# Dilated attention on tokens in order of their residues, and unsplit first modulation rows

## The chip, the cores and the metric

The kernel runs on one core of a Trainium2 chip as one program. The metric is the device time in microseconds, the median of several runs. Of the kernel before, three runs took 3383.66, 3390.68 and 3393.23 us.

## The reference, cut to what matters

The program is two transformer blocks one after the other over 512 tokens of width 1024, in float32. The first block has two layers, each with modulation by a condition vector, attention over 512 tokens and 256 context tokens, and a mixture of experts. The part of it that matters here is the first line: `silu` of two condition vectors (for tokens and for context) times 2048 columns of `mod_w[0]` gives a shift and a scale, and the layer begins with them.

```python
mods  = (silu_c  @ mod_w[i] + mod_b[i]).reshape(b, 1, 6, d)          # six rows of 1024
cmods = (silu_cc @ mod_w[i][:, :n_cm*d] + mod_b[i][:n_cm*d])         # the same for the context
a_lat = modulate(h_lat, mods[:, :, 0], mods[:, :, 1])                # x * (1 + scale) + shift
```

The second block normalises `x` to `h`, and feeds three branches with `h @ w_in`: gated linear attention, a short convolution, and dilated attention. Sigmoid gates `h @ w_gate + b_gate` weigh the branches; then come an output product and a feed-forward part.

```python
z = rmsnorm(x, pre_mix_g[l]) @ w_in[l]
y_gla, y_sc = gla_branch(...), sc_b * causal_dwconv(sc_c * sc_x, sc_conv_w[l])
y_dil = dilated_branch(d_q, d_k, d_v, positions)                     # 4 heads, 3 groups
gates = sigmoid(h @ w_gate[l] + b_gate[l]).reshape(B, S, 3, D_MODEL)
merged = sum(gates * einsum('bsgc,gcd->bsgd', [y_gla, y_sc, y_dil], w_branch[l]), axis=2)
```

Each head of the dilated branch has three groups, which are softmaxes of their own, joined by their denominators: one over near tokens (distances up to 128), and two over tokens whose distance is a multiple of four. `strided_window_attn` gathers the tokens of one residue modulo four with `t.reshape(B, L, dil, H, D).transpose(0, 2, 3, 1, 4)`.

## The kernel before, in words

Matrices lie with the inner dimension on the 128 partitions, so a width of 1024 is KC = 8 chunks. Most products are three matmuls (`mm3`, lines 239 to 243): each operand is split into a rounded part and a rest (`split`, L247 on ACT, L248 on DVE), and hi times hi, lo times hi and hi times lo are added in PSUM. `Stream` (from line 34) brings weights to raw slots by SP's DMA queue, in the order of a plan; a load into a slot waits until the slot was read. `get` gives split weights, `plain` unsplit ones.

The code makes instructions in program order, with generators that mix two bodies of work; a scheduler then sets the order on each engine from its own estimates. Each engine runs its list strictly in order.

At the start, `first_mods` (L326) reads 32 pieces of 256 KB of `mod_w` through 6 slots; each is split, and multiplied by the two condition columns in two matmuls (L339, L340). The row is copied out, transposed in 16 small pieces, and gives `mcol`, the shift and scale by partition (L349, L350). Then tokens `x` are transposed, modulated (L459, L460), and multiplied by the first attention weights `k_ab`, whose loads (L66) stand behind all pieces of `mod_w` in SP's queue.

In the second block `hTh` and `hTl` hold the split, transposed `h` (128 partitions x 8 chunks x 512 tokens). `gla` and `short_conv` run interleaved (`both`, L131), followed by `dilated`. There `project` makes, for the heads in pairs, V of each of three groups: for 128 tokens at a time, stationary operand `hTh[:, k, tokens]` or `hTl`, moving operand 256 weight columns, so 48 matmuls for each PSUM tile of 2 x 256 and 96 for each group and pair of heads. For groups 1 and 2 the tokens are `slice(b + i, 512, 4)`, every fourth one. Q and K are 128 x 512 tiles by head and group, turned by `rope_tables`. `scores(r)` handles the queries of residue r: one product with 512 keys (group 0, L2218) and two with 128 (L2220); with float32 operands each is two matmul instructions. `values(r)` writes the result into `yTh[:, h, r::4]`. After that gates and branches alternate: two gate tiles with a sigmoid (L1847) from PSUM, then two branch products `pb`; both kinds take PSUM tiles of tag `mm`, of which there are two.

Of the kernel before, what the change touches and what calls it, by code (L numbers as in the profile page):

```python
# [13 lines left out]
F32 = mybir.dt.float32  # L14
# [9 lines left out]
P = 128  # L24
D = 1024
# [158 lines left out]
class Kern:  # L184
# [121 lines left out]
    def silu_c(self, ps, pool, cr, sr):  # L306
# [7 lines left out]
        self.c2 = pool.tile([P, KC, 2, 2], FR, name="c2")  # L314
        c2 = pt[:, :16].rearrange("p (w k) -> p k w", w=2)
        self.split(self.c2[:, :, 0], self.c2[:, :, 1], c2)
# [10 lines left out]
    def first_mods(self, st, ps, row, cols):  # L327

        nc, A = self.nc, self.A
        pc = ps.tile([P, KC, 8], F32, tag="aux", name="pc")  # L330
        for j in (1, 0):
            nc.gpsimd.dma_start(row[4:5], A["mod_b"][0:1, j * D:(j + 1) * D])

            pm = [ps.tile([P, 512], F32, tag="mm", name="pm")[:4] for _ in range(2)]
            for k in range(KC):
                c = self.c2[:, k].rearrange("p x w -> p (x w)")
                for n in range(2):
                    h, l = st.get()
                    nc.tensor.matmul(pm[n], c, h[:, 0], start=k == 0, stop=False)  # L339
                    nc.tensor.matmul(pm[n][:2], c[:, :2], l[:, 0], start=False, stop=k == KC - 1)  # L340
                yield
            for n in range(2):
                nc.scalar.activation(row[:4, n * 512:(n + 1) * 512], pm[n], AF.Copy)
            for k in range(KC):
                self.transpose(pc[:, k, :5], row[:, k * P:(k + 1) * P])
            t = cols.rearrange("p (k c) -> p k c", k=KC)
            nc.scalar.activation(t, pc[:, :, :5], AF.Copy)
            m = self.mcol[:, 0, j]
            nc.vector.scalar_tensor_tensor(m, t[:, :, 0:2], float(j), t[:, :, 2:4], op0=OP.add, op1=OP.add)  # L349
            nc.vector.tensor_add(m, m, t[:, :, 4:5].to_broadcast([P, KC, 2]))  # L350
# [181 lines left out]
    def mixer_ab(self, atp, then):  # L532
        nc, tc, A, cp = self.nc, self.tc, self.A, self.cp
        NT, NB = NLAT + NCTX, 6
        with ExitStack() as es:
# [13 lines left out]
            wp = ws.enter_context(tc.tile_pool(name="m0w", bufs=1))  # L549
            plan = self.mod_plan(0, (1, 0))  # L550
# [13 lines left out]
            self.silu_c(ps, mp, xc[:16, 4096:4224], xc[:16, 4224:4352])  # L564
            st = Stream(self, wp, plan, 6, 6, 768)
            for i, _ in enumerate(self.first_mods(st, ps, xc[:5, 2048:3072], xc[:, 3072:3112])):
                if i == 12:
                    load_x(0)
# [1849 lines left out]
```

## Time and profile before

| | |
|---|---|
| runs | 3383.66, 3390.68, 3393.23 us |
| profiled execution | 3393.14 us, span 3391.4 us |
| busy | PE 90%, PEld 66%, DVE 45%, ACT 30%, POOL 17% |
| DMA | 647 MB, 191 GB/s on average |
| granted clock of PE, mean | 0.960 |

PE means matmuls, PEld the loads of the stationary operand, which overlap matmuls. A matmul's row shows its whole duration, but the next one starts before it ends; so the pace is read from the distance of two starts. In the rows a line number is the line of a helper where the helper makes the instruction: 241 to 243 are the three matmuls of every split product, told apart by their tiles. In the text below "k" is a chunk of 128 of the width. A row of the timeline ends with the idle time ahead of it and who ended that, where there was any.

### The profile page before, as it was taken

How to read it: one execution, taken by the hardware profiler on the slowest of the kernel's cores; microseconds unless marked ns; L12 is line 12 of the kernel's file. 1: busy time of each engine (PE TensorE's matmuls, PEld its weight loads, DVE VectorE, ACT ScalarE, POOL GpSimd, SP SyncE). 2: the span in 40 equal slices, each digit the busy share in tenths (PEclk: the TensorE clock that was granted, in tenths of full speed). 3: DMA queues.
4: the chain of work that ended last, by engine and by line, in shares of the span. 5: the costliest groups of instructions: out<-in, count | busy, mean ns of one | idle time of the engine just before them, and what ended most of it. 6: DMA issues, size and time to landing. Idle time of an engine off the chain costs nothing. (4 is left out here: it accounts for less than half of the span.)

```text
span 3391.4 us, 50303 instructions
## 1 busy us (share of the span) xinstructions
PE 3067.6 (90%) x18965; PEld 2233.6 (66%) x18965; DVE 1519.4 (45%) x3415; ACT 1010.7 (30%) x2201; POOL 592.6 (17%) x557
## 2 busy tenths in 40 slices
PE   7999999799999928998799989399999999979998
PEld 3677757455555527887555545188889888858887
DVE  5578866443222257755521212344533333365533
ACT  5455561111111015654111111133232332233321
POOL 1101012243422232011222111100031300010000
PEclk9999999799999968999799999799999999979999
DMA  7433142899999641113697999722121112412232
GB/s 255 157 99 105 62 165 106 350 393 418 392 418 419 283 145 34 51 42 116 265 399 288 418 417 403 263 85 73 46 75 50 69 63 93 150 75 100 100 118 75
DMA packets 146160, 647.13 MB, mean 191 GB/s; under 512 B 27890, under 2 KB 35586, under 8 KB 85586
## 3 DMA queue, kind: packets, MB, share of 16 engines
q1 hardware_dynamic: 120802, 597.84, 45.6%
q0 software_dynamic: 22224, 36.24, 3.4%
q10 hardware_dynamic: 2848, 9.19, 0.7%
q8 instruction: 186, 3.05, 0.4%
q14 instruction: 100, 0.82, 0.1%
HBM read 669.98 MB, written 35.03 MB: 208 GB/s over the span
## 5 line engine op out<-in xcount | busy, mean ns | idle before, releaser
L1597 PE MATMUL u<-raw,xs 128*64 128x256 f32 x5312 | 597.5, 382 | 18.9 <-DMA raw<-in_k_w 18.5
L1597 PEld LDWEIGHTS u<-raw,xs 128*64 128x64 f32 x5312 | 378.5, 137 | 219.1 <-DMA raw<-in_k_w 22.6
L248 DVE TENSOR_TENSOR wl<-raw,wh 128x2048 fp32r<-128x2048 f32 (+3 forms) x178 | 278.6, 1573 | 434.8 <-ACT wh L247 433.2
L247 ACT ACTIVATE wh<-raw 128x2048 fp32r<-128x2048 f32 (+3 forms) x180 | 239.1, 1335 | 416.1 <-PE pm L242 187.9
L241 PE MATMUL pm<-hTh,wh 128*128 128x512 f32 x872 | 344.8, 395 | 1.6 <-DVE hTl L248 1.4
L243 PE MATMUL pm<-hTh,wl 128*128 128x512 f32 x872 | 341.5, 392 | 1.1 <-DVE wl L248 1.1
L242 PE MATMUL pm<-hTl,wh 128*128 128x512 f32 x872 | 341.7, 392 | 0.0
L1617 PE MATMUL y<-raw,gs 128*64 128x512 f32 x1328 | 300.4, 598 | 4.2 <-ACT gs L1612 1.5
L1602 DVE TENSOR_TENSOR sg<-sg,u 128x256 f32<-128x256 f32 x132 | 55.5, 421 | 513.0 <-PEq L1650 293.4
L243 PE MATMUL pm<-wh,aTl 128*128 128x384 f32 (+2 forms) x576 | 201.1, 349 | 7.7 <-POOL aTl L461 7.5
L241 PE MATMUL pm<-wh,aTh 128*128 128x384 f32 (+2 forms) x576 | 203.5, 354 | 2.1 <-ACT aTh L460 2.0
L1617 PEld LDWEIGHTS y<-raw,gs 128*64 128x64 f32 x1328 | 88.9, 136 | 169.5 <-issue 155.4
L242 PE MATMUL pm<-wl,aTh 128*128 128x384 f32 (+2 forms) x576 | 198.8, 345 | 0.2 <-DVE wl L248 0.2
L1623 DVE SCALAR_TENSOR_TENSOR ys<-y,rt_sw,gate 128x512 f32<-128x512 f32 x128 | 93.5, 748 | 226.1 <-PE y L1617 226.1
L1601 ACT ACTIVATE sg<-u 128x256 f32<-128x256 f32 x132 | 50.6, 384 | 482.5 <-PE u L1597 315.8
L241 PEld LDWEIGHTS pm<-hTh,wh 128*128 128x128 f32 x872 | 163.9, 188 | 37.5 <-DVE hTl L248 1.8
L243 PEld LDWEIGHTS pm<-hTh,wl 128*128 128x128 f32 x872 | 163.6, 188 | 36.4 <-DVE wl L248 1.5
L242 PEld LDWEIGHTS pm<-hTl,wh 128*128 128x128 f32 x872 | 163.8, 188 | 34.5
L1612 ACT ACTIVATE gs<-t 128x512 f32<-128x512 f32 x66 | 39.4, 598 | 332.2 <-PE t L271 302.2
L1295 POOL DMA_INDIRECT xg<-f_d,rt_row x64 | 67.0, 1046 | 395.1 <-PE t L271 359.3
L271 PE MATMUL t<-ident,p 128*128 128x128 f32 x704 | 122.0, 284 | 6.0 <-ACT pT L885 1.0
L243 PEld LDWEIGHTS pm<-wh,aTl 128*128 128x128 f32 x576 | 114.3, 198 | 14.6 <-POOL aTl L461 9.2
(561 smaller groups left out, 5632.0 us busy)
## 6 DMA issues: line engine op xcount, KB each, us to landing
raw<-in_k_w SPq DMA_DIRECT2D x408, 1024.0 KB
raw<-in_k_sb SPq DMA_DIRECT2D x79, 1024.0 KB
raw<-in_mod_w SPq DMA_DIRECT2D x192, 256.0 KB
raw<-in_k_ab SPq DMA_DIRECT2D x24, 384.0 KB
raw<-in_k_cd SPq DMA_DIRECT2D x24, 384.0 KB
raw<-in_k_w_out SPq DMA_DIRECT2D x8, 1024.0 KB
raw<-in_k_sb SPq DMA_DIRECT2D x12, 512.0 KB
f_d<-f POOLq DMA_DIRECT2D x10, 512.0 KB, 2.9
```

What stands on the lines that cost most here:

```text
L241: nc.tensor.matmul(out, lh, rh, start=start, stop=False)
L242: nc.tensor.matmul(out, lh, rl, start=False, stop=False)
L243: nc.tensor.matmul(out, ll, rh, start=False, stop=stop)
L247: self.nc.scalar.activation(h, x, AF.Copy)
L248: (sub or self.nc.vector).tensor_sub(l, x, h)
L271: self.nc.tensor.transpose(out, in_, self.ident[:k, :k])
L1295: self.nc.gpsimd.indirect_dma_start(out=x, out_offset=None, in_=self.f_d[:nb * P], in_offset=bass.IndirectOffsetOnAxis(ap=gi, axis=0), bou ...
L1597: nc.tensor.matmul(pu[c][i][64 * n:64 * n + 64], xs[:, k, tok], w[:, k % 4, n * 256:(n + 1) * 256], start=k == 0, stop=k == KC - 1)
L1601: nc.scalar.activation(sg[c], pu[c][0], AF.Silu)
L1602: nc.vector.tensor_mul(sg[c], sg[c], pu[c][1])
L1617: nc.tensor.matmul(py[c][64 * n:64 * n + 64], gs[:, c, k % 2, k // 2], W[k // 2][:, k % 2, n * 512:(n + 1) * 512], start=k == 0, stop=k == 3)
L1623: nc.vector.scalar_tensor_tensor(y, py[c], sw[:, 0], gate[:, 0], op0=OP.mult, op1=OP.mult)
```

## The change

There are two parts. In the first, the 2048 columns for the first modulation come as 8 pieces of 1 MB, laid out ahead of time (`k_mod`), through 5 slots in a pool of its own. They are used unsplit in float32, with four column groups of 32 rows by 256 columns (`mod_row`, L325 to 329). The bias comes by POOL's DMA queue, and the row is transposed in two pieces. The pool of the six slots for `k_ab` opens after that pool is closed and covers its memory. In the second part, `hTh` and `hTl` are brought into the order of residues in place: each chunk is copied to a spare tile `turn` with a strided read, and back; `hTh` on ACT and `hTl` on POOL, in four further steps of `short_conv`. V of groups 1 and 2 and the queries of `scores` then take contiguous tokens; positions and masks follow that order (the masks lie where `gla` had its V), and the sigmoid of the gates, which still works on `h`, writes its result back to the natural order, with a stride of four. The writes to `yTh` stay.

```diff
@@ -324,30 +322,36 @@
-    def first_mods(self, st, ps, row, cols):
+    def mod_row(self, pm, k, w, last):
+
+        for q in range(4):
+            self.nc.tensor.matmul(pm[q * 32:q * 32 + 32], self.c2f[:, 2 * k:2 * k + 32], w[:, q * 256:(q + 1) * 256],
+                                  start=k == 0, stop=k == last)
+
+    def first_mods(self, ps, pool, then):
...
+        bias = pool.tile([P, 2, KC], F32, name="bias")
+        nc.gpsimd.dma_start(bias, A["k_mod_b"])
+        st = Stream(self, pool, [(Flat(A["k_mod"][i], 2),) for i in range(8)], 5, 0)
         for j in (1, 0):
-            nc.gpsimd.dma_start(row[4:5], A["mod_b"][0:1, j * D:(j + 1) * D])
-
-            pm = [ps.tile([P, 512], F32, tag="mm", name="pm")[:4] for _ in range(2)]
+            pm = ps.tile([P, 512], F32, tag="mm", name="pm")[:, :256]
             for k in range(KC):
-                c = self.c2[:, k].rearrange("p x w -> p (x w)")
-                for n in range(2):
-                    h, l = st.get()
-                    nc.tensor.matmul(pm[n], c, h[:, 0], start=k == 0, stop=False)
-                    nc.tensor.matmul(pm[n][:2], c[:, :2], l[:, 0], start=False, stop=k == KC - 1)
-                yield
-            for n in range(2):
-                nc.scalar.activation(row[:4, n * 512:(n + 1) * 512], pm[n], AF.Copy)
-            for k in range(KC):
-                self.transpose(pc[:, k, :5], row[:, k * P:(k + 1) * P])
-            t = cols.rearrange("p (k c) -> p k c", k=KC)
-            nc.scalar.activation(t, pc[:, :, :5], AF.Copy)
-            m = self.mcol[:, 0, j]
-            nc.vector.scalar_tensor_tensor(m, t[:, :, 0:2], float(j), t[:, :, 2:4], op0=OP.add, op1=OP.add)
-            nc.vector.tensor_add(m, m, t[:, :, 4:5].to_broadcast([P, KC, 2]))
+                if k % 2 == 0:
+                    w = st.plain()
+                self.mod_row(pm, k, w[:, k % 2], KC - 1)
+            row = pool.tile([P, 256], F32, tag="row", name="row", bufs=2)
+            nc.scalar.activation(row, pm, AF.Copy)
+            pc = ps.tile([P, 512], F32, tag="aux", name="pc")
+            for c in range(2):
+                self.transpose(pc[:, c * P:(c + 1) * P], row[:, c * P:(c + 1) * P])
+
+            for c in range(2):
+                m, b = (v.rearrange("p (q c) w -> p c q w", c=2)[:, c] for v in (self.mcol[:, 0, j], bias[:, j, :, None].to_broadcast([P, KC, 2])))
+                nc.vector.scalar_tensor_tensor(m, pc[:, c * P:(c + 1) * P].rearrange("p (q x) -> p q x", q=4)[:, :, 0:2], float(j), b,
+                                               op0=OP.add, op1=OP.add)
+            if j:
+                then()
@@ -546,8 +550,7 @@
             ws = ent(ExitStack())
-            wp = ws.enter_context(tc.tile_pool(name="m0w", bufs=1))
-            plan = self.mod_plan(0, (1, 0))
+            plan = []
@@ -562,10 +565,10 @@
             self.silu_c(ps, mp, xc[:16, 4096:4224], xc[:16, 4224:4352])
+            with tc.tile_pool(name="m0f", bufs=1) as fp:
+                self.first_mods(ps, fp, lambda: load_x(0))
+            wp = ws.enter_context(tc.tile_pool(name="m0w", bufs=1))
             st = Stream(self, wp, plan, 6, 6, 768)
-            for i, _ in enumerate(self.first_mods(st, ps, xc[:5, 2048:3072], xc[:, 3072:3112])):
-                if i == 12:
-                    load_x(0)
             for b in range(1, NB):
@@ -1844,7 +1847,7 @@
                             gt = gp.tile([P, 512], F32, tag="gt", name="gt")
-                            nc.scalar.activation(gt, pm, AF.Sigmoid, bias=bg[:, g * 8 + d0 + i:g * 8 + d0 + i + 1])
+                            nc.scalar.activation(gt.rearrange("p (i r) -> p r i", r=4), pm.rearrange("p (r i) -> p r i", r=4), AF.Sigmoid, bias=bg[:, g * 8 + d0 + i:g * 8 + d0 + i + 1])
                             gts.append(gt)
@@ -1981,6 +1984,14 @@
                 self.split(yTh[:, i0 + i], yTl[:, i0 + i], t)
+                yield
+
+        for k in range(KC):
+            for x, (h, copy) in enumerate(((self.hTh, lambda o, i: nc.scalar.activation(o, i, AF.Copy)), (self.hTl, nc.gpsimd.tensor_copy))):
+                t = sp.tile([P, 512], FR, tag=f"turn{x}", name="turn", bufs=1)
+                copy(t.rearrange("p (r i) -> p r i", r=4), h[:, k].rearrange("p (i r) -> p r i", r=4))
+                copy(h[:, k], t)
+            if k % 2:
                 yield
@@ -2147,9 +2158,10 @@
             d2 = ent(tc.tile_pool(name="dl2", bufs=2))
-            mask0 = dp.tile([P, 515], F32, name="mask0")
+
+            masks = mp.tile([P, 4, 512], F32, tag="V", name="masks").rearrange("p b n -> p (b n)")
+            mask0, mask1 = masks[:, :7 * P].rearrange("p (r i) -> p r i", r=7), masks[:, 7 * P:9 * P]
             nc.sync.dma_start(mask0, A["k_dmask0"])
-            mask1 = dp.tile([P, 256], F32, name="mask1")
             nc.sync.dma_start(mask1, A["k_dmask1"])
@@ -2162,7 +2174,7 @@
                 nc.sync.dma_start(pi, self.bcast_rows(psrc, 512))
-                nc.vector.tensor_copy(pos, pi)
+                nc.vector.tensor_copy(pos.rearrange("p (r i) -> p r i", r=4), pi.rearrange("p (i r) -> p r i", r=4))
                 nc.vector.tensor_scalar(pos, pos, inv[:, 0:1], None, op0=OP.mult)
@@ -2187,7 +2199,7 @@
                         for i in range(2):
-                            proj(w, slice((b + i) * P, (b + i + 1) * P) if g == 0 else slice(b + i, 512, 4), pm, i * 256)
+                            proj(w, slice((b + i) * P, (b + i + 1) * P), pm, i * 256)
                         nc.scalar.activation(V[:, g, b:b + 2], pm.rearrange("p (b e) -> p b e", b=2), AF.Copy)
@@ -2214,12 +2226,12 @@
                     s = ps.tile([P, 768], F32, tag="s", name="s")
-                    tok = slice(r, 512, 4)
+                    tok = slice(r * P, (r + 1) * P)
                     nc.tensor.matmul(s[:, 0:512], QK[0, 0][:, tok], QK[0, 1], start=True, stop=True)
                                          start=True, stop=True)
-                    nc.vector.tensor_add(s[:, 0:512], s[:, 0:512], mask0[:, 3 - r:515 - r])
+                    nc.vector.tensor_add(s[:, 0:512], s[:, 0:512], mask0[:, 3 - r:7 - r].rearrange("p r i -> p (r i)"))
                     nc.vector.tensor_add(s[:, 512:768], s[:, 512:768], mask1)
```

Three places in the order of the instructions changed. The first is SP's queue at the start. Before, the last pieces of `mod_w` for the first modulation were followed by `k_ab` and `x`:

```order
L73 DMA raw_140<-in_mod_w 128x512
L73 DMA raw_141<-in_mod_w 128x512
L66 DMA raw_142<-in_k_ab 128x768
L562 DMA xl<-in_x 128x1024
L66 DMA raw_143<-in_k_ab 128x768
L66 DMA raw_144<-in_k_ab 128x768
L66 DMA raw_145<-in_k_ab 128x768
L73 DMA raw_140<-in_mod_w 128x512
L73 DMA raw_141<-in_mod_w 128x512
L73 DMA raw_142<-in_mod_w 128x512
L562 DMA xl<-in_x 128x1024 x3
```

Now, from the fifth of the 8 pieces on (`xl` are token blocks of `x`; `raw_237` is the first slot of the pool that opens later):

```order
L66 DMA raw_143<-in_k_mod 128x2048
L66 DMA raw_139<-in_k_mod 128x2048
L66 DMA raw_140<-in_k_mod 128x2048
L66 DMA raw_141<-in_k_mod 128x2048
L565 DMA xl<-in_x 128x1024 x3
L66 DMA raw_237<-in_k_ab 128x768
L66 DMA raw_238<-in_k_ab 128x768
L66 DMA raw_239<-in_k_ab 128x768
L66 DMA raw_240<-in_k_ab 128x768
L73 DMA raw_241<-in_mod_w 128x512
L73 DMA raw_242<-in_mod_w 128x512
```

Three blocks of `x` moved ahead of `k_ab`, and the first load of `k_ab` waits for the readers and writers of the memory that it covers, up to the end of `first_mods`.

The second place is PE at the end of `gla`, where V of group 0 of the dilated branch (`pm`, 128x256) stands among the products of the linear attention (`po`, `pz`). Before:

```order
L242 MATMUL pm_27315<-wl_27040,hTh_25529 128x256
L243 MATMUL pm_27315<-wh_27039,hTl_25530 128x256
L241 MATMUL pm_27315<-wh_27039,hTh_25529 128x256
L242 MATMUL pm_27315<-wl_27040,hTh_25529 128x256
L243 MATMUL pm_27315<-wh_27039,hTl_25530 128x256
L241 MATMUL pm_27315<-wh_27039,hTh_25529 128x256
L242 MATMUL pm_27315<-wl_27040,hTh_25529 128x256
L243 MATMUL pm_27315<-wh_27039,hTl_25530 128x256
L2105 MATMUL po_27166<-state_27160,qkT_26022 128x128
L2103 MATMUL po_27166<-V_25531,ST_26020 128x128
```

Now (`pm_27201` is the first PSUM tile of V, `pm_27251` the second):

```order
L243 MATMUL pm_27201<-wh_26878,hTl_25369 128x256
L241 MATMUL pm_27201<-wh_26878,hTh_25368 128x256
L242 MATMUL pm_27201<-wl_26879,hTh_25368 128x256
L243 MATMUL pm_27201<-wh_26878,hTl_25369 128x256
L241 MATMUL pm_27251<-wh_26878,hTh_25368 128x256
L242 MATMUL pm_27251<-wl_26879,hTh_25368 128x256
L241 MATMUL pm_27201<-wh_26878,hTh_25368 128x256
L242 MATMUL pm_27201<-wl_26879,hTh_25368 128x256
L243 MATMUL pm_27201<-wh_26878,hTl_25369 128x256
L243 MATMUL pm_27251<-wh_26878,hTl_25369 128x256
L2116 MATMUL po_27017<-state_26999,qkT_25861 128x128
L2114 MATMUL po_27017<-V_25370,ST_25859 128x128
```

Before, seven chunks of the first 128 tokens stood ahead of the first product with `state`; now six chunks do, with the first chunk of the second tile between them. They read what the copies write.

The third place is ACT in the same stretch; `qkT` is what the `pz` products read, and `turn` is the spare tile. Before:

```order
L247 ACTIVATE wh_27039<-raw1_25520 128x2048
L1970 ACTIVATE u_26981<-pm_26983 128x512
L247 ACTIVATE yh_25999<-t_26809 128x512
L247 ACTIVATE wh_27310<-raw0_25519 128x2048
L2092 ACTIVATE qkT_26022<-pt_27140 128x512
L2107 ACTIVATE O_27146<-po_27148 128x2x128 x2
L247 ACTIVATE yh_25999<-t_26860 128x512
L2107 ACTIVATE O_27146<-po_27166 128x2x128 x2
```

Now:

```order
L1990 ACTIVATE turn_27039<-hTh_25368 128x512
L1990 ACTIVATE hTh_25368<-turn_27039 128x512
L1990 ACTIVATE turn_27045<-hTh_25368 128x512
L1990 ACTIVATE hTh_25368<-turn_27045 128x512
L1990 ACTIVATE turn_27073<-hTh_25368 128x512
L247 ACTIVATE wh_27196<-raw0_25358 128x2048
L2103 ACTIVATE qkT_25861<-pt_26979 128x512
L2118 ACTIVATE O_26985<-po_26987 128x2x128 x2
L1990 ACTIVATE hTh_25368<-turn_27073 128x512
L1990 ACTIVATE turn_27079<-hTh_25368 128x512
L1990 ACTIVATE hTh_25368<-turn_27079 128x512
L1990 ACTIVATE turn_27099<-hTh_25368 128x512
```

Four copies of two chunks and the beginning of a fifth now stand ahead of the split of a weight piece and of `qkT`. On POOL, which was idle here before, the copies of `hTl` stand ahead of the squares of `O`:

```order
L1993 COPY hTl_25369<-turn_27076 128x512
L1992 COPY turn_27082<-hTl_25369 128x512
L1993 COPY hTl_25369<-turn_27082 128x512
L1992 COPY turn_27102<-hTl_25369 128x512
L1993 COPY hTl_25369<-turn_27102 128x512
L1992 COPY turn_27108<-hTl_25369 128x512
L1993 COPY hTl_25369<-turn_27108 128x512
L2134 TENSOR_TENSOR sq_27002<-O_26985 128x512
```

## Rows read from the trace of the kernel before

**Rows 1.** Page, busy time by engine, and GB/s in 40 slices.

```profile
PE 3067.6 (90%) x18965; PEld 2233.6 (66%) x18965; DVE 1519.4 (45%) x3415; ACT 1010.7 (30%) x2201; POOL 592.6 (17%) x557
...
GB/s 255 157 99 105 62 165 106 350 393 418 392 418 419 283 145 34 51 42 116 265 399 288 418 417 403 263 85 73 46 75 50 69 63 93 150 75 100 100 118 75
```

**Rows 2.** Timeline of PE, V of groups 1 and 2: start, duration, operation.

```profile
2444.22 0.40 PE L243 MATMUL pm<-wh,hTl 128*128 128x256 f32 x1
2444.46 0.40 PE L241 MATMUL pm<-wh,hTh 128*128 128x256 f32 x1
```

**Rows 3.** Timeline of PE, V of group 0.

```profile
2421.98 0.28 PE L241 MATMUL pm<-wh,hTh 128*128 128x256 f32 x1
2422.10 0.28 PE L242 MATMUL pm<-wl,hTh 128*128 128x256 f32 x1
```

**Rows 4.** Weight loads, 2412 to 2426 us (group 0): count | busy, mean ns.

```profile
L241 PEld LDWEIGHTS pm<-wh,hTh 128*128 128x128 f32 x14 | 2.7, 191 | 0.2 <-issue 0.2
```

**Rows 5.** Weight loads, 2434 to 2479 us (groups 1 and 2).

```profile
L241 PEld LDWEIGHTS pm<-wh,hTh 128*128 128x128 f32 x64 | 21.3, 333 | 0.9 <-ACT V L2191 0.9
```

**Rows 6.** Windows: V of groups 1 and 2, head 0; the gates.

```profile
2433.70:2479.50 45.80, 45.80 (x194) 45.75 (x195) 10.81 (x14) 8.40 (x10) 0.00 (x0) 1.00 0.17 60
2748.00:2950.00 202.00, 201.15 (x876) 163.98 (x875) 73.97 (x72) 57.39 (x56) 0.00 (x0) 1.00 0.32 110
```

**Rows 7.** Timeline of PE around one score product.

```profile
2527.94 1.60 PE L2244 MATMUL po<-pT,V 128*128 128x128 f32 x12
...
2530.32 1.02 PE L2218 MATMUL s<-qk 128*128 128x512 f32 x2
...
2531.17 1.09 PE L2220 MATMUL s<-qk 128*128 128x128 f32 x4
...
2531.90 0.59 PE L241 MATMUL pm<-hTh,wh 128*128 128x512 f32 x1
```

**Rows 8.** Timeline of PE, last projection of the convolution, first state product.

```profile
2398.37 0.40 PE L243 MATMUL pm<-hTh,wl 128*128 128x512 f32 x1
...
2410.86 0.37 PE L2105 MATMUL po<-state,qkT 64*128 64x128 f32 x1 [0.17 <-DVE state L2120]
```

**Rows 9.** Timeline of ACT, tail of the linear attention.

```profile
2399.98 0.63 ACT L247 ACTIVATE yh<-t 128x512 fp32r<-128x512 f32 x1 [12.88 <-DVE t L1982]
...
2404.70 1.91 ACT L247 ACTIVATE wh<-raw 128x2048 fp32r<-128x2048 f32 x1 [4.09 <-PE pm L242]
...
2406.52 0.58 ACT L2092 ACTIVATE qkT<-pt 128x512 f32<-128x512 f32 x1
```

**Rows 10.** Groups of POOL: count | busy, mean ns.

```profile
L248 POOL TENSOR_TENSOR wl<-raw,wh 128x2048 fp32r<-128x2048 f32 x2 | 9.0, 4518 | 0.2 <-ACT wh L247 0.2
...
L2123 POOL TENSOR_TENSOR sq<-O 128x512 f32<-128x512 f32 x4 | 5.4, 1362 | 63.1 <-ACT O L2107 63.1
```

**Rows 11.** Groups of ACT: the same copy, strided and contiguous result.

```profile
L247 ACT ACTIVATE yh<-po 128x128 fp32r<-128x128 f32 x16 | 6.4, 400 | 19.8 <-PE po L2244 19.8
...
L247 ACT ACTIVATE oh<-po 128x128 fp32r<-128x128 f32 x16 | 4.4, 277 | 15.5 <-PE po L485 15.5
```

**Rows 12.** Timeline of ACT, first pair of gates.

```profile
2766.77 0.67 ACT L1847 ACTIVATE gt<-pm,bg 128x512 f32<-128x512 f32 x1
```

**Rows 13.** Timeline of PE, first pair of gates.

```profile
2767.74 0.39 PE L241 MATMUL pb<-yh,wh 128*128 128x512 f32 x1
```

**Rows 14.** Timeline of SP's queue, start.

```profile
2.23 30.33 SPq L73 DMA_DIRECT2D raw<-in_mod_w  x32
...
32.93 0.33 SPq L66 DMA_DIRECT2D raw<-in_k_ab  x1
```

**Rows 15.** Waits of SP's queue, 0 to 60 us: total, times, longest.

```profile
SPq L73 <- DVE wl L248: 15.1, 25, 1.7
```

**Rows 16.** Timeline of PE, start.

```profile
43.62 1.07 PE L366 MATMUL pm<-raw,c2f 128*32 128x256 f32 x4 [1.71 <-DMA raw<-in_mod_w]
44.61 0.69 PE L241 MATMUL pm<-wh,aTh 128*128 128x384 f32 x1
```

More of the change, by code (lines that the diff above doesn't have):

```diff
@@ L313, in silu_c @@
         self.transpose(pt[:, :16], sr)
-        self.c2 = pool.tile([P, KC, 2, 2], FR, name="c2")
         c2 = pt[:, :16].rearrange("p (w k) -> p k w", w=2)
-        self.split(self.c2[:, :, 0], self.c2[:, :, 1], c2)
         self.c2f = cp.tile([P, 2 * KC + 30], F32, name="c2f")
@@ L325, in mod_plan @@
                 for j in rows for k in range(KC) for c in range(j * D, (j + 1) * D, 512)]
-    def first_mods(self, st, ps, row, cols):
+    def mod_row(self, pm, k, w, last):
[3 more added lines that the diff above has]
+    def first_mods(self, ps, pool, then):
         nc, A = self.nc, self.A
-        pc = ps.tile([P, KC, 8], F32, tag="aux", name="pc")
+        bias = pool.tile([P, 2, KC], F32, name="bias")
+        nc.gpsimd.dma_start(bias, A["k_mod_b"])
+        st = Stream(self, pool, [(Flat(A["k_mod"][i], 2),) for i in range(8)], 5, 0)
@@ L1787, in second_body @@
             self.hTl = hTl = hp.tile([P, KC, 512], FR, tag="hl", name="hTl")
-            V = hp.tile([P, 4, 512], F32, name="V")
+            V = hp.tile([P, 4, 512], F32, tag="V", name="V")
             with tc.tile_pool(name="sbx", bufs=2) as xp:
@@ L1830, in second_body @@
             y.append(y_tiles("sby2"))
-            self.dilated(*y[2], ps)
+            self.dilated(*y[2], ps, hp)
             mp = ent(tc.tile_pool(name="sbm", bufs=1, side="right"))
@@ L2138, in gla, with dilated @@
                 self.split(yTh[:, h], yTl[:, h], pt)
-    def dilated(self, yTh, yTl, ps):
+    def dilated(self, yTh, yTl, ps, mp):
         nc, tc, A = self.nc, self.tc, self.A
@@ L2302, in constants @@
     gm[:, 7], gm[:, 8], gk[:, 7] = u <= t, u > t, u == t
-    d = 4 * u + 3 - np.arange(515)[None, :]
+    d = 4 * (u - t)[:, None, :] + 3 - np.arange(7)[None, :, None]
     dmask0 = np.where((d >= 0) & (d <= 128), 0, NEG).astype(f)
@@ L2406 @@
     data["k_bg"] = by_part(data.pop("b_gate_2"))[:, :, 0]
+    data["k_mod"] = np.concatenate([pieces(data["mod_w"][0][:, j * D:(j + 1) * D], 2, D) for j in (1, 0)])
+    data["k_mod_b"] = np.ascontiguousarray(data["mod_b"][0, :2 * D].reshape(2, KC, P).transpose(2, 0, 1))
     data.update(constants())
```

## The prediction

> **What bounds the kernel now.** I read the page first: TensorE is busy for 3067.6 of 3391.4 us (90%), and the DMA moves 418 GB/s in its full slices but 62 to 165 in slices 2 to 7 [rows 1]. So a change counts where PE or what feeds it gets shorter. Then I read the timeline of PE where the change acts. In V of groups 1 and 2 of the dilated branch the matmuls start 0.24 us apart [rows 2], in V of group 0, the same product with contiguous tokens, 0.12 us apart [rows 3]. The groups by form say which half is slow: the load of the stationary operand takes 191 ns with contiguous tokens [rows 4] and 333 ns with every fourth token [rows 5]. In head 0's stretch PE and PEld are both busy for all of 45.80 us [rows 6]: nothing but this pace sets its length, and neither ACT nor DVE nor the DMA (60 GB/s) is near its limit. At the start of the program it is otherwise: SP issues the 32 pieces of the first modulation over 30.33 us, the first weights of the attention leave at 32.93 [rows 14], and the first real product starts at 44.61 [rows 16]. SP waited 25 times, 15.1 us together, for DVE to have split a piece [rows 15].
>
> **V of groups 1 and 2.** Removed: the stride in 2 groups x 2 pairs of heads x 96 = 384 stationary loads. The starts of neighbours are 2444.46 - 2444.22 = 0.24 apart, and over the 48 products of a tile the pace is a little less: 192 products in 45.80 us less 0.5 us of gap give 0.236. Contiguous it is 0.120. That is 384 x (0.236 - 0.120) = 44.5 us. The first pair of heads lies in a stretch in which PE does nothing else; the second pair is mixed with the attention of head 1. There, something else could wait once the filling is shorter. I take the whole, **-44.5**; the bounds are -36 (a fifth is lost to new waits for the softmax chain) and -46. Feeding is enough: 96 products then take 11.5 us, in which ACT needs 1.91 us for the split of a piece [rows 9], and 1 MB in 11.5 us is 91 GB/s against 418.
>
> The Trainium skill says in "SBUF — State Buffer", section "Door 1: The DMA port swizzle (why `[64,N]` ≈ `[32,N]`)", that SBUF lines hold 16 bytes and that accesses want at least two hits in a line, and that one can stride for free up to 4 float32. Read by its second half, a stride of four would cost nothing and this part would be worth 0; the rows, with 333 against 191 ns, bear out the first half only.
>
> **Scores.** Of a score, the product with 512 keys starts at 2530.32, the four short ones at 2531.17 and the next work at 2531.90 [rows 7]. The short ones take 0.73 / 4 = 0.18 us each, where twelve contiguous float32 products of the same width take about 0.12 (1.60 us with the last one's 0.28 of tail). That is 0.25 for a score, with the first load of the long product perhaps 0.28, and 16 scores: -4.5. Some of it will be given back to the rotation on POOL that feeds scores; I take **-4**, bounds 0 and -5.
>
> **The copies into the new order.** No row shows a strided read on ACT or a copy on POOL. For ACT, a contiguous copy from SBUF is 0.63 [rows 9]. A strided result costs 400 against 277 ns for 128 columns [rows 11], so 0.12 for 128 and 0.49 for 512; a strided read is taken at the same, 1.1 us, with bounds 0.6 (nothing) and 1.9 (the longest ACT row here). For POOL the nearest rows are the subtraction over 2048 columns, 4.518 us or 1.13 for 512, and the square at 1.36 [rows 10]; I take 1.0 for a copy that reads one operand, bounds 0.5 and 2.3. The first chunk's outward copies stand early in the program, where both engines are idle. The rest cannot begin before the last projection of the convolution has read the chunk: chunk 0 is read at 2398.37 + 0.40 [rows 8]. On ACT, in the order shown: chunk 0 back at 2399.4, chunk 1 by 2401.4 (its reader ends later), the split of yh 0.63, chunks 2 and 3 at 1.7 each to 2405.4, chunk 4 outward to 2406.5, then the split of a weight 1.91 and qkT 0.58 to 2409.0, two evictions of O to 2410.3, chunk 4 back 2410.9, chunk 5 at 2412.6. POOL, at 1.0 a copy, ends chunk 5 at 2398.8 + 11 x 1.0 = 2409.8, so ACT is the later. On PE six chunks of V stand ahead of the first product with `state`, which started at 2410.86 [rows 8]; now it starts after chunk 5, at about 2413.1. The late qkT (2409.0 instead of 2407.1) gives about 2412.5 for the same product, and does not add. Who waits behind it is the rest of the linear attention and all that follows; chunks 6 and 7 are ready before PE comes to them. So **+2.3**; bounds 0 (the scheduler's filling swallows it) and +8.
>
> The Trainium skill's "GPSIMD Engine Reference", section "7. Performance pitfalls for Q7 kernels", lets a read with a step over 8 bytes cost half as much again; no row here shows one. By it the outward copies on POOL would take 1.5 us and chunk 5 would be ready at 2398.8 + 6 + 5 x 1.5 = 2412.3, still before ACT, and the sum is unchanged.
>
> **The gates.** The sigmoid reads PSUM in order and writes with a stride of four. By rows 11 that adds 4 x 0.123 = 0.49 to its 0.67 [rows 12]. The second sigmoid of the first pair then ends at 2766.77 + 0.67 + 0.49 = 2767.93. The branch product that takes its PSUM tile (two tiles of the tag) started at 2767.74 [rows 13], so PE waits some 0.24. Gates come in 12 groups, alike but for the last: 11 x 0.24 = **+2.6**, in a stretch in which PE is busy for 201.15 of 202 us [rows 6], so it is paid. Bounds 0 (a stride on the write side is cheaper from a 512-wide instruction) and +6 (0.49 each time).
>
> **Positions, masks.** The strided copy of the positions is one DVE instruction beside V on PE; masks take the memory of `gla`'s V, which is free before SP comes to them. Nothing, as long as the tables are ready before the first Q; if not, Q's rotation waits, not its product.
>
> **The start.** 32 splits on ACT and DVE, 64 matmuls, 16 transposes go; 64 matmuls of another form, 4 transposes come. Data is the same, 8.4 MB. At 418 GB/s it takes 20.1 us, at the first slice's average of 255 [rows 1] 33. Issue begins at 2.23; with some 2 us to land, the last piece is there between 24 and 37. Without 25 waits for the split it is nearer the fast end: 27. Its 8 matmuls take 2.1 (4 in 1.07 [rows 16]), and the eviction, two transposes and two small DVE operations about 1.5, an estimate from 0.58 for a copy on ACT [rows 9]. So `mcol` stands at 30.5. Now SP's wait: the first load of `k_ab` covers the memory of the first pool, so it leaves at 30.5, before at 32.93. Behind it in the queue are all further weights and three blocks of `x`; PE has nothing else. But three blocks of `x` stand ahead of it, so transposes and modulation are done while it flies. Before, 11.7 us lay between that issue and the first product; now I take 2 for the landing, 1.9 for the split in both halves and 0.5, so the first product starts at 35: **-9**. Bounds -13 (everything at full rate) and +2 (pieces at 255 GB/s and most of the 11.7 us again).
>
> **Sum.** -44.5 - 4 + 2.3 + 2.6 - 9 = -52.6. From the profiled execution, 3393.1 (span 3391.4 and 1.7 around it), that is 3340.5. It lies 2.4 above the median of the three runs, 3390.7; against that median the forecast is **3338 us**. The ends of the terms do not fall together; adding the likelier half of them, the forecast's own range is 3327 to 3349.
>
> **Rivals.**
> A. The start gives nothing: `k_ab` goes out only when the pool is closed, and the pieces land slowly. For it: no load can hide the wait now. Against it: SP has no other waits left. Without the -9: 3347, and with both ends of the copies 3352.
> B. The copies are slower than their nearest rows and the tail of the linear attention waits for chunk 5: at +8 the time is 3344; at 2.3 us for each POOL copy chunk 5 stands at 2424.1 and the product with `state` some 13.7 late: 3349.
> C. The pace of V is not the stride's: the split products of groups 1 and 2 would stay at 0.236, as would scores. For it: only that PE, too, shows 0.40 for each. Against it: group 0 has the same shapes and halves the pace. Then -9 + 2.3 + 2.6 = -4: 3387. (By the second half of the rule on SBUF lines that the Trainium skill gives, cited above, it would come so.)
> D. Slower than before: POOL's copies of `hTl` are several times slower than its arithmetic. PE stands at chunk 7 at about 2421 in the old time, and 15 copies after 2398.8 must be done: with p for a copy the delay is 2398.8 + 15p - 2421. All other terms give -54.9; so from p = 5.1 us on the change loses, and at 6 us the delay is 67.8 and the time 3390.7 + 12.9 = 3404. Against it: 1.13 and 1.36 for the same width with two operands.
>
> **Chances.** Forecast 0.75, A 0.12, B 0.08, C 0.03, D 0.02. The range for 8 in 10 takes the forecast's own and A and B as far as 3356: 3324 to 3356. This kernel's measurement tells 0.3%, about 10 us, from no change; A and B stay far beyond it on the fast side, C is within, D is slower by more: faster 0.95, same 0.03, slower 0.02.
>
> **What would show it.** In the changed profile: products of V in all groups 0.12 apart and loads near 190 ns; the four short score products 0.12 apart; a wait of PE of about 2 us at V's chunk 5 ahead of the first `state` product, ended by ACT's copy; sigmoids of 1.16 us and 0.2 us of idle PE at the second branch product; first attention product near 35 us, with SP's wait for the last `mcol` near 30. I am wrong if V shortens by less than 36 us, if the end of `gla` grows by over 8, or if the first product starts after 42.

## The result

Four runs of the changed kernel took 3344.18 to 3350.43 us, median 3344.95; four of the kernel before 3383.66 to 3393.23, median 3389.83. The ratio is 0.9869, with a 95% interval of 0.9855 to 0.9883: 44.9 us, or 1.3%, faster. The forecast was 3338, its range 3324 to 3356. From the page of the changed kernel, busy times and granted clock (in tenths) in 40 slices of 83.6 us:

```profile
PE 3016.8 (90%) x19017; PEld 2180.2 (65%) x19017; DVE 1502.2 (45%) x3382; ACT 1015.6 (30%) x2180; POOL 608.1 (18%) x572
...
PEclk9999999799999968999799999889899999989999
```

PE is busy 51 us less [rows 1]. Slice 29, from 2340 to 2424 us, has an 8 in the clock; before, it had a 9. It holds the tail of the linear attention, and that is where the term lies that I had made too small.

To see where the time came from I compare the two traces place by place: the start of the same instruction in both, the later kernel's lead in us. The first column is the changed kernel, the others are the experiments told below. Each lead rests on one profiled execution and on starts read to 0.1 us, so its last digit can be off by one.

| place | changed | first part only | copies left out | one copy | one copy, DVE | V strided | gates not turned back | gates by DVE | both |
|---|---|---|---|---|---|---|---|---|---|
| first attention unit, L496 | 8.7 | 8.8 | 7.5 | 7.8 | 9.3 | 9.2 | 8.7 | 9.0 | 8.4 |
| convolution, first L1963 | 11.9 | 9.4 | 12.9 | 10.4 | 13.0 | 8.7 | 7.5 | 10.6 | 12.3 |
| first state product, L2105 | 9.5 | 9.4 | 12.9 | 6.2 | 7.6 | 6.8 | 5.0 | 8.7 | 6.8 |
| first V evicted, L2191 | 1.4 | 9.4 | 12.9 | 6.2 | 7.5 | -1.5 | -3.2 | 0.5 | 6.7 |
| last value product, L2244 | 51.2 | 9.6 | 62.9 | 56.1 | 57.1 | 5.5 | 46.7 | 50.4 | 56.3 |
| first output row, L1941 | 46.9 | 9.6 | 58.6 | 51.5 | 52.8 | 1.1 | 46.6 | 49.7 | 55.6 |

From row to row the differences are the terms. The lead of the start is 8.7 us after the first unit. Up to the convolution, in code that both kernels share, the lead moves by -1.2 to +5.4 from one execution to another. This is drift between executions (the profiled one of the kernel before took 3393.14 us, 3.3 above the median), and the reason why only differences within the second block are read to a microsecond. Then the tail of the linear attention takes 10.5 back, the dilated attention gives 49.8, the gates take 4.3.

**V and scores.** The timeline of PE in V of group 1, the weight loads of V (groups 1 and 2; count | busy, mean ns), and the window of head 0's V:

```profile
2440.03 0.28 PE L241 MATMUL pm<-wh,hTh 128*128 128x256 f32 x1
2440.15 0.28 PE L242 MATMUL pm<-wl,hTh 128*128 128x256 f32 x1
```

```profile
L241 PEld LDWEIGHTS pm<-wh,hTh 128*128 128x128 f32 x40 | 7.7, 192 | 0.0
```

```profile
2432.43:2455.20 22.77, 22.77 (x190) 22.77 (x191) 10.88 (x14) 8.30 (x9) 0.00 (x0) 1.00 0.31 104
```

The pace is 0.120 instead of 0.236 and the load 192 instead of 333 ns [rows 2, 5]; what took 45.80 us takes 22.77 [rows 6]. A score on PE:

```profile
2505.99 1.02 PE L2230 MATMUL s<-qk 128*128 128x512 f32 x2
2506.85 0.61 PE L2232 MATMUL s<-qk 128*128 128x128 f32 x4
2507.21 0.48 PE L241 MATMUL pm<-hTh,wh 128*128 128x512 f32 x1
```

The four short products now take 2507.21 - 2506.85 = 0.36 instead of 0.73 us [rows 7].

**The start.** SP's queue, SP's wait for the modulation (total, times, longest), and PE:

```profile
2.21 15.75 SPq L66 DMA_DIRECT2D raw<-in_k_mod  x8
...
32.54 1.75 SPq L66 DMA_DIRECT2D raw<-in_k_ab  x4
```

```profile
SPq L66 <- DVE mcol L351: 6.8, 1, 6.8
```

```profile
37.95 0.69 PE L241 MATMUL pm<-wh,aTh 128*128 128x384 f32 x1 [2.00 <-ACT wh L247]
```

All pieces are issued by 18.0 instead of 32.6 us, `k_ab` waits 6.8 us for the last `mcol` and leaves at 32.54, almost when it did [rows 14]; but transposes and modulation are done by then, and the first product comes at 37.95 instead of 44.61 [rows 16].

**The tail of the linear attention.** The timeline of PE, idle time and its end in brackets, then two rows of the same stretch before, and windows after (busy by engine PE, PEld, DVE, ACT, POOL, then granted clock, DMA share and GB/s):

```profile
2397.14 0.88 PE L2124 MATMUL pz<-V,qkT 128*64 128x128 f32 x12 [1.38 <-ACT qkT L2103]
...
2400.06 0.39 PE L241 MATMUL pm<-wh,hTh 128*128 128x256 f32 x1 [0.31 <-ACT hTh L1990]
...
2401.01 0.50 PE L243 MATMUL pm<-wh,hTl 128*128 128x256 f32 x2 [0.46 <-POOL hTl L1993]
2401.45 0.48 PE L2116 MATMUL po<-state,qkT 64*128 64x128 f32 x2
...
2408.38 0.79 PE L2116 MATMUL po<-state,qkT 64*128 64x128 f32 x2 [0.90 <-DVE state L2129]
...
2411.28 0.79 PE L2116 MATMUL po<-state,qkT 64*128 64x128 f32 x2
2412.00 0.79 PE L2114 MATMUL po<-V,ST 128*128 128x128 f32 x2
...
2419.23 0.58 PE L243 MATMUL pm<-wh,hTl 128*128 128x256 f32 x1
```

```profile
2411.28 0.49 PE L2103 MATMUL po<-V,ST 128*128 128x128 f32 x2
...
2421.04 0.39 PE L243 MATMUL pm<-wh,hTl 128*128 128x256 f32 x1
```

```profile
2396.00:2400.00 4.00, 2.60 (x25) 2.23 (x25) 3.52 (x3) 3.94 (x7) 3.87 (x2) 1.00 0.03 6
...
2404.00:2408.00 4.00, 3.49 (x16) 2.22 (x14) 1.97 (x3) 1.18 (x3) 2.98 (x4) 0.50 0.01 2
```

```profile
2402.60:2423.06 20.46, 19.57 (x68) 14.53 (x67) 6.18 (x16) 3.28 (x8) 6.39 (x7) 0.50 0.11 39
```

PE waits 1.38 us for qkT, 0.31 for chunk 5 of hTh, 0.46 for a chunk of hTl; in 2396 to 2400 it is busy for 2.60 of 4 us. The first state product is 2.4 us later than before, relative to what precedes (lead 11.9 to 9.5). But then the granted clock is 0.50, which is 1.2 of its 2.4 GHz, and stays there from 2402.6 to 2423.1, until V's products have run again for some 4 us: the state products start 0.72 apart (2411.28, 2412.00) in place of 0.42, and the block from 2401.45 to 2419.23 takes 17.8 us, where the same products took 10.2 before, from 2410.86 [rows 8] to 2421.04. That is 7.6 of the 10.5 us. Most of the 7.6 is the clock; 0.90 is one more wait, at 2408.38, for DVE's `state`. DVE had itself waited 4.33 us for a square on POOL, which stood behind POOL's last copies. Why all of these were late is seen on ACT, POOL and DVE:

```profile
2390.00 1.11 ACT L1990 ACTIVATE turn<-hTh 128x512 fp32r<-128x512 f32 x1
2391.14 0.63 ACT L1990 ACTIVATE hTh<-turn 128x512 fp32r<-128x512 f32 x1
...
2396.50 0.60 ACT L2103 ACTIVATE qkT<-pt 128x512 f32<-128x512 f32 x1
```

```profile
2392.53 1.14 POOL L1992 CAST turn<-hTl 128x512 fp32r<-128x512 f32 x1
2393.73 0.62 POOL L1993 CAST hTl<-turn 128x512 fp32r<-128x512 f32 x1
...
2396.70 3.23 POOL L1992 CAST turn<-hTl 128x512 fp32r<-128x512 f32 x1
```

```profile
2384.81 0.75 DVE L1983 SCALAR_TENSOR_TENSOR v<-u,cw,v 128x512 f32<-128x512 f32 x1
...
2394.73 1.44 DVE L1983 SCALAR_TENSOR_TENSOR v<-u,cw,v 128x512 f32<-128x512 f32 x1
...
2396.64 2.29 DVE L248 TENSOR_TENSOR wl<-raw,wh 128x2048 fp32r<-128x2048 f32 x1 [0.48 <-ACT wh L247]
...
2406.03 0.69 DVE L2135 TENSOR_REDUCE ss<-sq 128x4 f32<-128x512 f32 x1 [4.33 <-POOL sq L2134]
```

ACT's copies cost 1.11 outward and 0.63 back, and qkT ends at 2397.1 behind them. On POOL the contiguous copy takes 0.62, the strided one 1.14 here, and 3.23 where DVE splits a weight: that copy starts with the split and ends 1.0 us after it. DVE pays as well: the same step of the convolution takes 0.75 us with POOL idle and 1.44 beside POOL's copies. It does not take a stride for that: the kernel before has it too, beside a square on POOL from 2407.72 to 2410.05 that reads and writes contiguously:

```profile
2409.07 1.53 DVE L1981 SCALAR_TENSOR_TENSOR v<-u,cw,v 128x512 f32<-128x512 f32 x1
```

**The gates.** One pair on ACT, on PE, and the waits of PEld in the gates:

```profile
2715.85 1.17 ACT L1850 ACTIVATE gt<-pm,bg 128x512 f32<-128x512 f32 x1
```

```profile
2716.59 0.40 PE L243 MATMUL pb<-yh,wl 128*128 128x512 f32 x1
2717.07 0.50 PE L241 MATMUL pb<-yh,wh 128*128 128x512 f32 x1
```

```profile
PEld pb L241 <- ACT gt L1850: 6.6, 12, 0.7
```

The sigmoid takes 1.17, as forecast. The second branch product starts 0.48 after its predecessor, 0.25 more than the usual 0.23; but there are twelve such waits, 6.6 us of the loads together, and the longest is 0.7.

### The profile page after: what moved, and what is told of

It is laid out like the page before. It is cut to its first block, busy times and chain, and to the rows that moved or that the text cites. A ratio compares the mean times of both kernels' runs of the same rounds, so it can differ in the third digit from the quotient of the medians.

```text
span 3343.4 us, 50272 instructions
## 1 busy us (share of the span) xinstructions
PE 3016.8 (90%) x19017; PEld 2180.2 (65%) x19017; DVE 1502.2 (45%) x3382; ACT 1015.6 (30%) x2180; POOL 608.1 (18%) x572
## 5 line engine op out<-in xcount | busy, mean ns | idle before, releaser
L248 DVE TENSOR_TENSOR wl<-raw,wh 128x2048 fp32r<-128x2048 f32 (+3 forms) x146 | 257.3, 1768 | 392.3 <-ACT wh L247 391.5
L247 ACT ACTIVATE wh<-raw 128x2048 fp32r<-128x2048 f32 (+3 forms) x148 | 219.3, 1487 | 390.9 <-PE pm L242 178.0
```

What stands on the lines that cost most here:

```text
L247: self.nc.scalar.activation(h, x, AF.Copy)
L248: (sub or self.nc.vector).tensor_sub(l, x, h)
```

## The experiments

All times are compared with runs of the kernel before, 3389.4 us on those chips; the interval is that of the ratio. The table above has the leads. The intervals of one copy, of odd chunks on DVE and of the two versions of the gates overlap with the changed kernel's, 0.9855 to 0.9883; so what these four are worth is read from the leads, not from the times.

**The first part alone** (the hunks of `first_mods` and its caller on the kernel before).

> The kernel before with the first part alone: the first modulation from unsplit 1 MB pieces; the second block as before. Theory: the first product of the attention comes at 38 us instead of 44.6, and what the two traces show as a lead of 12.0 us at the end of the first block is all of this part's: 3389.8 - 12 = 3378 (3375 to 3381). Rival: only the lead of 8.7 us that stands after the first attention unit (at about 122 us) belongs to it, and the rest is a difference from one execution to the next: 3381 to 3384. Second rival: the lead is eaten in the expert stage, where transfers set the pace: over 3386.

Median 3378.84; ratio 0.9967 (0.9957 to 0.9977), 8 to 15 us faster. By the median that is the theory's range; but in its trace the lead is 8.8 after the first unit and 9.3 to 9.9 through the whole second block, as the first rival has it. The runs leave 9 to 11 us for this part; by the first rival's reading some of the 12 in the changed kernel's profile was drift.

**The copies left out** (the loop over `turn` does nothing but yield).

> The changed kernel with the copies into the order of residues left out (so the dilated attention and the gates work on tokens in the wrong order). Theory: the tail of the linear attention loses all of the 10.5 us that the traces show it grew by: no wait of PE for qkT, hTh or hTl, granted clock 1.00 throughout the state products, which take 10 us instead of 18; 3345 - 10.5 = 3334.5. Rival: the clock falls there for another reason (less work on PE around it), and only the 2.5 us of waits go: 3342.5, with the clock at 0.50 behind the first state product as now.

Median 3331.71; ratio 0.9828 (0.9811 to 0.9844). The lead is 12.9 ahead of the tail and 12.9 behind it. A window of its tail:

```profile
2404.00:2408.00 4.00, 4.00 (x21) 2.90 (x20) 0.69 (x1) 0.66 (x2) 1.04 (x1) 1.00 0.00 0
```

The clock is 1.00 throughout. All of the 10.5 us, waits and clock, come from the copies. (The time is 13 us below the changed kernel's; the tail explains 10.5 of them, and the rest is no more than executions differ.)

**One copy instead of two.**

```diff
-            self.hTh = hTh = hp.tile([P, KC, 512], FR, tag="hh", name="hTh")
+            hh = [hp.tile([P, KC + 1, 512], FR, tag="h" + x, name="hT" + x) for x in "hl"]
+            self.hTh, self.hTl = hTh, hTl = [h[:, 1:] for h in hh]
...
-                copy(t.rearrange("p (r i) -> p r i", r=4), h[:, k].rearrange("p (i r) -> p r i", r=4))
-                copy(h[:, k], t)
+                copy(h[:, k].rearrange("p (r i) -> p r i", r=4), h[:, k + 1].rearrange("p (i r) -> p r i", r=4))
...
+        self.hTh, self.hTl = hh[:, :KC], hl[:, :KC]
```

> The changed kernel with one copy for each chunk instead of two: hTh and hTl have a ninth place; h lies in places 1 to 8, and chunk k goes in the new order to place k, which the chunk before it has left; the cosine table lies beside the masks to make room. Theory (lateness of the copies starves PE, and the starved PE loses its clock): chunk 5 is ready about 5 us earlier, PE waits for none of them, the clock stays at 1.00 and the tail is as before the change: 3335 (3333 to 3338). Rival (it is their work beside DVE and ACT that costs, in whatever order): half of it goes, 3340. Second rival: the strided copies still come late and the clock still falls: 3345.

Median 3340.12; ratio 0.9853 (0.9837 to 0.9870). The tail takes 4.2 us back instead of 10.5. PE, ACT and windows:

```profile
2400.16 1.26 PE L2125 MATMUL pz<-V,qkT 128*64 128x128 f32 x12 [2.85 <-ACT qkT L2104]
...
2402.80 0.41 PE L242 MATMUL pm<-wl,hTh 128*128 128x256 f32 x1
2403.01 0.41 PE L243 MATMUL pm<-wh,hTl 128*128 128x256 f32 x1
...
2404.70 0.48 PE L2117 MATMUL po<-state,qkT 64*128 64x128 f32 x2
```

```profile
2392.03 5.78 ACT L1992 ACTIVATE hTh<-hTh 128x512 fp32r<-128x512 f32 x5
2397.72 1.89 ACT L247 ACTIVATE wh<-raw 128x2048 fp32r<-128x2048 f32 x1
2399.53 0.58 ACT L2104 ACTIVATE qkT<-pt 128x512 f32<-128x512 f32 x1
```

```profile
2400.50:2403.90 3.40, 3.40 (x22) 3.07 (x19) 3.40 (x4) 0.15 (x1) 2.11 (x1) 0.50 0.31 41
2403.92:2408.00 4.08, 4.08 (x28) 3.10 (x28) 2.18 (x6) 0.90 (x2) 0.00 (x0) 1.00 0.55 227
```

No chunk is late any more, but all of ACT's copies and the split of a weight now stand ahead of qkT, so PE's one wait is 2.85 us, longer than all of those before together. Still the cost is less. The clock falls here too, right behind the wait, but it stays at 0.50 for only 3.4 us (2400.5 to 2403.9), while V's products run; the state products begin after it and keep their 0.42. In the changed kernel it stays there for 20.5 us (2402.6 to 2423.1), with the state products in them. The loss for each product is much the same: at 0.50 V's products start 0.21 apart (2402.80, 2403.01) instead of 0.12, the state products 0.72 instead of 0.42. So the 10.5 us come neither from the length of the waits alone nor from the kind of product that meets the low clock, but from how long the clock stays low. The other profiles have the same two lengths in this tail: 20.5 us in the three further kernels with two copies, 3.4 us in the two further ones with one copy. What makes the one or the other, no run here shows. The expected 3335 was wrong in that the lateness of the chunks was not the only lateness: qkT was one, too.

**Odd chunks of hTh on DVE** (the edit against the run before).

```diff
-            for h, copy in ((hh, lambda o, i: nc.scalar.activation(o, i, AF.Copy)), (hl, nc.gpsimd.tensor_copy)):
+            for h, copy in ((hh, nc.vector.tensor_copy if k % 2 else lambda o, i: nc.scalar.activation(o, i, AF.Copy)), (hl, nc.gpsimd.tensor_copy)):
```

> The changed kernel with one copy for each chunk (nine places, as in the run before), and the copies of hTh for odd chunks on DVE instead of ACT. In that run all copies were done in time but five of them stood on ACT ahead of qkT, for which PE then waited 2.85 us, and its clock fell for 4 us. Theory: with three copies of ACT gone, qkT comes about 3 us earlier, PE waits under 1 us and keeps its clock; the tail loses 4 us more: 3336 (3334 to 3338). Rival: DVE, which makes the state and the split of the weight there, is now late by as much: 3340.

Median 3339.12; ratio 0.9858 (0.9841 to 0.9874): no change against the run before. The tail takes 5.5 us. ACT, then DVE and PE:

```profile
2392.40 1.13 ACT L1992 ACTIVATE hTh<-hTh 128x512 fp32r<-128x512 f32 x1 [4.33 <-PE pt L271]
2395.03 1.11 ACT L1992 ACTIVATE hTh<-hTh 128x512 fp32r<-128x512 f32 x1 [1.50 <-DVE hTh L1993]
...
2397.85 0.58 ACT L2104 ACTIVATE qkT<-pt 128x512 f32<-128x512 f32 x1
```

```profile
2390.78 1.52 DVE L1993 CAST hTh<-hTh 128x512 fp32r<-128x512 f32 x1
...
2396.17 0.63 DVE L1993 CAST hTh<-hTh 128x512 fp32r<-128x512 f32 x1 [1.24 <-ACT hTh L1992]
```

```profile
2398.48 0.88 PE L2125 MATMUL pz<-V,qkT 128*64 128x128 f32 x12 [3.86 <-ACT qkT L2104]
```

Each copy writes the place that the copy before it has read, so the chain passes from ACT to DVE and back, and ACT's copy at 2395.03 waits 1.50 for DVE's. qkT is no earlier than in the run before, and PE waits 3.86. DVE begins its first copy of the tail at 2390.78, although POOL could begin the copy of the same chunk of `hTl` at 2385.74: until then DVE works at its own list. Then it takes 1.52 us for it beside POOL's copies, where a later one takes 0.63 with POOL done. So it is the rival, in time and in kind: DVE is late, though behind other work than the state and the split, and ACT waits for it.

**V from every fourth token again** (the slice of before for groups 1 and 2).

> The changed kernel with V of groups 1 and 2 taken from every fourth token again (which is the wrong order there); all else as changed, the scores too. Theory: the pace goes back to 0.237 us for 384 products: 3345 + 44.5 = 3389.5. Rival: beside the attention of the second pair of heads PE had slack, so that only head 0's half is paid in full: 3345 + 36 = 3381. Second rival: the pace was not the stride's: 3345.

Median 3386.37; ratio 0.9986 (0.9976 to 0.9996). PE in V:

```profile
2450.02 0.40 PE L241 MATMUL pm<-wh,hTh 128*128 128x256 f32 x1
2450.25 0.40 PE L242 MATMUL pm<-wl,hTh 128*128 128x256 f32 x1
```

The pace is 0.23 to 0.24 again. From the first V to the last value product this kernel gains 5.5 + 1.5 = 7.0 on the kernel before, the changed one 49.8. So V is worth 42.8, with both pairs of heads paid in full or nearly so, and the scores and what hangs on them 7.0.

**The gates not turned back** (sigmoid with `gt`, `pm` in plain order).

> The changed kernel with the gates' sigmoid writing in PSUM's order (the gates then stand in the order of residues and meet products in the natural order, which leaves out the way back). Theory: the sigmoid falls from 1.17 to 0.68 us, PE waits for no PSUM tile in the gates, and all of the 4.3 us that the traces show between the end of the dilated attention and the output product goes: 3345 - 4.3 = 3340.7. Rival: PE's waits there come from other work (weights, DVE), and nothing goes: 3345.

Median 3339.01; ratio 0.9852 (0.9836 to 0.9869). The lead is 46.7 at the end of the dilated attention and 46.6 behind the gates: the whole 4.3 is the sigmoid's stride.

**The gates turned back by DVE** (the sigmoid in plain order; the product of the first branch likewise).

```diff
-                                nc.vector.tensor_mul(gt, gt, pb)
-                                nc.vector.tensor_add(acc[:, i], acc[:, i], gt)
+                                m = gp.tile([P, 512], F32, tag="m", name="m")
+                                nc.vector.tensor_mul(m.rearrange("p (i r) -> p i r", r=4), gt.rearrange("p (r i) -> p i r", r=4), pb.rearrange("p (i r) -> p i r", r=4))
+                                nc.vector.tensor_add(acc[:, i], acc[:, i], m)
```

> The changed kernel with the order of the gates turned back by DVE instead of ACT: the sigmoid writes in order, and DVE's product with the branch reads the gate contiguously in the order of residues, reads pb and writes its result with a stride of four. Theory: it is the sigmoid that holds the PSUM tile, and DVE has time (74 us of 202 busy before), so the gain is that of the kernel without the way back: 3340.7. Rival: DVE now holds the tile of pb longer, by as much as ACT did, and the wait only moves: 3345 or more.

Median 3340.84 (3332.90 to 3344.70); ratio 0.9854 (0.9835 to 0.9873). In the gates 0.7 us of lead is lost instead of 4.3. DVE's product (count | busy, mean ns):

```profile
L1863 DVE TENSOR_TENSOR m<-gt,pb 128x512 f32<-128x512 f32 x16 | 17.3, 1080 | 0.0
```

It takes 1.08 us (0.68 in the changed kernel), and PE hardly waits for it: 1.2 us at the last group, where the changed kernel waits 0.8, and 0.4 once before. So the theory holds by the leads; the times alone, 3332.90 to 3344.70, do not tell it from the changed kernel's.

**Both together** (one copy with the odd chunks on DVE, gates turned back by DVE).

> Both together: one copy for each chunk with the odd chunks of hTh on DVE, and the gates turned back by DVE. Theory: the two places are 280 us apart and add: 3345 - 9 - 4.3 = 3331.7, about 1% below the changed kernel's 3345 less noise of 3 us. Rival: one of them gives nothing, 3336 to 3341.

Median 3335.30, 3329.10 to 3337.80, ratio 0.9839 (0.9823 to 0.9855): all four runs lie below all four of the changed kernel (from 3344.18), though the intervals of the two ratios touch at 0.9855. The tail takes 5.6 us, the gates 0.7. The time lies between the theory and the rival. The two places add, but the theory counted 9 us for the copies, and this way of copying gives back only about 5.

## Why the prediction was right, and where it was not

- **V, -44.5.** Right in place and mechanism; measured 42.8. The slack beside the second pair's attention that I feared did not show.
- **Scores, -4.** Measured 7.0 for all of the dilated attention but V's pace, beyond my bound of 5. The short products alone save 16 x 0.37 = 6 us; I had taken 0.12 for their pace from products of the values, and they reach 0.09. What the last microsecond is, no run separates.
- **Start, -9.** Measured 9 (8.7 and 8.8 after the first unit in the two kernels with this part as it is). The first product came at 38, not 35: `mcol` was 2 us later than I had it, and the split of `k_ab` later, too. Two more us are in the lead up to the first unit, which I had not counted. They come late, between 105 us (lead 7.3) and 116 us: there the kernel before waits 2.0 us for pieces of `mod_w` (the changed one 1.3), and its clock is at 0.50 for 3.4 us from 112.4 on (1.00 in the changed one). Whether the change makes this difference is not shown; that the sum came out at 9 is in part luck.
- **Copies, +2.3: the step that failed.** The delay I had worked out came in size: the first state product is 2.4 us later, against 2.3. Its path was another. I had one wait at chunk 5, ended by ACT, and a late qkT that "does not add"; the trace has 1.38 for qkT, 0.31 for chunk 5 and 0.46 for POOL's copy of `hTl`. That the sizes agree is in part luck. Above all, "So +2.3; bounds 0 ... and +8" took the wait for the whole cost. It left out that PE's clock falls after such waits and stays at half for 20.5 us. With one more wait of 0.90 for DVE this costs 7.6 us more, so that the tail grew by 10.5, beyond the bound of 8 that I had named as a sign of being wrong. My rival B gave 3344, nearly the time that came, but by copies slower than their rows. ACT's were as forecast (1.11 to 1.18), and of POOL's only one was far slower, 3.23; so that agreement is luck.
- **The gates, +2.6.** Measured 4.3, by the mechanism forecast (without the stride it is gone). I had sized the wait from one pair, 0.24, for 11 groups; twelve waits of the loads, 6.6 us together, cost PE 4.3.
- Rivals C and D did not come. The sum of the terms measured, -49.8 + 10.5 + 4.3 - 9 = -44.0, is close to the change in the medians, -44.9. By the terms the forecast was 8.6 us too low (7 by the medians): the copies and the gates cost 9.9 more than forecast and V gave 1.7 less, the scores and what hangs on them gave 3 more.

The rule of the Trainium skill in "SBUF — State Buffer", section "Door 1: The DMA port swizzle (why `[64,N]` ≈ `[32,N]`)", by which one can stride for free up to 4 float32, does not hold here for loads of the stationary operand. Between the changed kernel and the run with V strided nothing else differs, and the pace is 0.120 against 0.23 to 0.24, the load 192 against 330 ns. For POOL the Trainium skill in "GPSIMD Engine Reference", section "7. Performance pitfalls for Q7 kernels", has half as much again for a strided read; here it was 1.08 against 0.62 with DVE idle, and up to 1.66, once 3.23, with DVE at work.

What stays open is why the clock stayed low for 20.5 us in the kernels with two copies and for 3.4 in those with one. The runs show that it fell behind the waits, that it came back within V's products in both, and that it never fell there without the copies; they don't show what makes the difference. And a version in which qkT is not behind any copy was not made. With one copy the tail still loses 4.2 to 5.6 us, without copies none, so it could be worth up to 5 us more.

## What to carry to other kernels

Here a stationary operand with a stride of four float32 halved the pace of matmuls with 128 and 256 columns, and one pass of copies over 32 KB a partition paid for many uses of it. Where a new wait is put on PE, its price is not its length alone: look at the granted clock behind it, and at how long it stays low. When an order has to be turned back at the end, give it to an engine that holds nothing up while doing so.

## What the runs showed of the hardware that was not expected

- After waits of 2.2 us in all, the granted clock was 0.50 from 2402.6 to 2423.1, although PE was busy for 19.57 of 20.46 us there; after one wait of 2.85 us with V's products behind it, it was back at 1.00 about 4 us later.
- A step of DVE on 128x512 took 1.9 times as long beside POOL's copies (1.44 instead of 0.75), with no operand in common, and 1.53 beside a contiguous square on POOL; POOL's copy took 3.23 instead of 1.1 beside DVE's split.
- A product on DVE with three operands, two of which have a stride of four, costs 1.08 instead of 0.68 us.
